# Shared keys and values in a windowed attention: two passes of the weighted sum, scores in one piece, and the lower halves of the weights made by accumulating transfers

## Chip, cores and metric

One NeuronCore of a Trainium2 chip runs the whole program in one launch. The metric is the device time of one execution in microseconds (us); the median of the runs shown counts. All data are float32.

## What is computed

Two hybrid layers and then one block of another kind, on 512 tokens of width 1024. Nearly all of the work is products with weight matrices. The part that the change rewrites is the windowed attention of the two hybrid layers: 16 query heads of 64 columns share 4 heads of keys and values (four query heads each), and a block of 128 queries sees its own block of keys and its two neighbours:

```
q = rms_norm(z_q.reshape(B, S, 16, 64)); k = rms_norm(z_k.reshape(B, S, 4, 64))   # then rotary on 16 columns
s = einsum('bnqhgd,bnjhd->bhgnqj', qb, kwin) / 8        # kwin: blocks n-1, n, n+1
s = where(|kpos - qpos| <= 128 and inside, s, -1e30)
m = max(max(s), sink); p = exp(s - m); p = p / (sum(p) + exp(sink - m))
o = einsum('bhgnqj,bnjhd->bnqhgd', p, vwin) * silu(gate)
```

## The kernel before

**Products.** TensorE multiplies in a rounded form of float32 (float32r). So that little is lost, each operand x is split into a high part hi (x rounded) and a low part lo = x - hi, and a product is three matmuls into the same PSUM tile: hi by hi, hi by lo, lo by hi. `mm3` does that; its three lines are L172, L173 and L174. Moving operands are 512 columns wide nearly everywhere.

**Weights.** All weight matrices come as a stream of 509 chunks of 128 rows by 1024 columns (512 KB), in the order of their use. `_load_raw` has the SyncE queue (SP) fetch one into a buffer `raw`; `_split_next` makes `hi` by a copy on ScalarE (ACT, L149) and `lo` by a subtraction on VectorE (DVE, L150). Each of `raw`, `hi` and `lo` has WB = 3 buffers, and `take`, called for each block of weights, keeps the splitting two chunks ahead of the use. A chunk holds eight blocks, and one block with 512 moving columns is three matmuls, so a chunk is 24 matmuls of 512 columns in most stages ("the steady rate"). Where a stage works on two token tiles only (`halves` in `tm`, the first tiles in `norm_tokens`, `down`), a chunk is used up in half of that or less. Some chunks (`HOLD`) are split into other tiles and kept.

**Attention.** For each layer there are two cores, one for each half g of the heads. `att_core` goes through eight steps, (n, pp) for the four query blocks n and two groups of four heads. A step issues: the weighted sum of the step before last (V, `mm3` with both heads of the half in one tile of 128 columns, three matmuls for each key block, results `pi`), the transposes of the step before (L771, four for each key block, results `pi`), and the scores of this step (L792, twelve matmuls of 64 rows; two that follow each other use the upper and the lower 64 rows of the array, results `pa`), then the masked maximum (L794, DVE), four exponentials (L223, ACT), and the scaling (L217 on DVE, L223 on ACT). There are 2, 3, 3 and 2 key blocks for the four n. PSUM has four `pa` banks, two `pi` banks and two `pm` banks. `weave` lets one unit of other work (one call of `fm`, 24 matmuls into `pm`: the first product of the convolution branch) go before each step. In the second core of a layer, filter taps of the convolution (`conv_taps`, DVE, L213) run along in the background.

**Order.** A scheduler orders each engine's instructions by the order of the program and by what it reckons to be ready; each engine then works through its own list in that order, waiting at semaphores. `issue_after(i)` adds the rule that an instruction of the same engine comes behind i in that list.

Of the kernel before, what the change touches and what calls it, by code (L numbers as in the profile page):

```python
# [10 lines left out]
F32 = mybir.dt.float32  # L11
F32R = mybir.dt.float32r
# [53 lines left out]


class Kern:
    def __init__(self, ctx, tc, ap):
# [21 lines left out]
        self.first = {}  # L91
        self.bg = None
# [39 lines left out]
    def _split_next(self):  # L132
# [36 lines left out]

    def mm3(self, out, lh, ll, rh, rl, start, stop):  # L170
# [3 lines left out]
        T.matmul(out, lhsT=ll, rhs=rh, start=False, stop=stop)  # L174

    def fm(self, key, cols, rhs, blocks=None, ts=None, pool=None):
# [4 lines left out]
        for k, (rh, rl) in enumerate(rhs):  # L181
# [3 lines left out]
            self.mm3(ps, wh, wl, rh, rl, k == 0, k == len(rhs) - 1)  # L185
# [489 lines left out]

    def att_kv(self, l, xg, xs):
# [3 lines left out]
        self.rms_h(xs, self.vk("norm_g", l), range(KT // 2))  # L680
        self.av = []
        for i in range(2):
            h, lo = self.slot(F32R), self.slot(F32R)
            for j in range(2):
                t = 2 * i + j
                c = slice(j * 256, j * 256 + 256)
                r = self.r[:, t:t + 1]
                self.act(h[:, c], ps[t][:, 256:512], AF.Copy, scale=r)
                self.stt(lo[:, c], ps[t][:, 256:512], r, h[:, c].bitcast(F32), ALU.mult, ALU.subtract)
            self.av.append((h, lo))  # L690
# [6 lines left out]
    def att_kT(self, nrm, ks):  # L697
        yield from nrm
        self.kT = []
        for p in range(2):  # L700
            self.kT.append(self.att_T(ks, p))
            yield
# [36 lines left out]
    def att_core(self, l, g):  # L739


        T = self.T
        qT, kT, av, sg = self.qT, self.kT[g], self.av, self.asg
        by_b = lambda x: x.rearrange("q (b p) -> q b p", b=2)
        sink, nsink = (by_b(x[:, 8 * g:8 * g + 8]) for x in (self.vk("sink", l), self.nsink))
        ya = [self.slot() for _ in range(4)]
        iters = [(n, pp) for n in range(NT) for pp in range(2)]
        hss = [slice(0, 64), slice(64, 128)]
        s1, s2 = {}, {}
        for it in range(len(iters) + 2):  # L750
            if 0 <= it - 2:
                n, pp = iters[it - 2]
                pt = s2.pop(it - 2)
                ps = self.misc()
                for x, (jb, ph, pl) in enumerate(pt):
                    c = (jb % 2) * 256 + g * 128
                    vh, vl = av[jb // 2]
# [795 lines left out]
```

## Time and profile before

| what | value |
|---|---|
| median of 3 runs | 3069.0 us (3067.52 to 3069.83) |
| profiled execution, its own time | 3067.16 us |
| its span, first to last instruction | 3065.4 us |
| TensorE clock granted over the span | 0.998 of full speed |
| PE busy | 3022.8 us |
| DVE busy | 2078.2 us |
| ACT busy | 1130.5 us |
| POOL (GpSimd) | 0.2 us, 4 instructions |
| HBM traffic | 94 GB/s over the span |

PE is TensorE's matmuls, PEld its weight loads. Matmuls overlap in the pipeline, so one is listed as taking about 0.39 us although the next one starts much sooner; what a matmul costs is read from the starts in the timeline. Idle time of an engine other than the one that sets the end costs nothing by itself. Some matmul records can be missing from a trace, so a group's count can be a few short; the counts of matmuls that matter are worked out from the loops.

### The profile page before, as it was taken

Reading aid. Unit: us, or ns where it says so; the run is one execution under the profiler, and the core shown is the slowest. Engines: PE = TensorE matmul, PEld = TensorE weight load, DVE = VectorE, ACT = ScalarE, POOL = GpSimd, SP = SyncE. Lnnn points to the kernel's source line nnn. Section 1 sums busy time; section 2 is a strip of 40 time slices with the busy share of each in tenths; the row PEclk is TensorE's granted clock in tenths of the full one; section 3 lists DMA queues with packets and bytes.
Section 4 is the critical chain, followed back from the end, with each engine's and each line's share of the span. In section 5 each row is a group of like instructions: output and inputs, shape, how many; then the busy total and the mean of one; then the engine's idle time right before and its main releaser. Section 6 shows DMA issues by size and latency. Waiting matters only on the chain.

```text
span 3065.4 us, 36069 instructions
## 1 busy us (share of the span) xinstructions
PE 3022.8 (99%) x13996; PEld 2470.4 (81%) x13996; DVE 2078.2 (68%) x3787; ACT 1130.5 (37%) x1783; POOL 0.2 (0%) x4
## 2 busy tenths in 40 slices
PE   8999999999999999999999999999999999999998
PEld 6777888887888877788888788887888888788887
DVE  7778897877444776889787764467776754753326
ACT  4545223334233444532333433333543332422222
POOL 0000000000000000000000000000000000000000
PEclk9999999999999999999999999999999999999999
DMA  4121322221233321122222132254222223422234
GB/s 163 63 69 49 97 89 76 83 76 63 95 98 129 117 76 62 62 83 97 71 74 76 63 103 96 97 173 143 90 90 69 65 74 123 161 96 99 98 110 151
DMA packets 83980, 288.99 MB, mean 94 GB/s; under 512 B 9440, under 2 KB 9696, under 8 KB 83680
## 3 DMA queue, kind: packets, MB, share of 16 engines
q1 hardware_dynamic: 83808, 286.68, 28.3%
q8 instruction: 110, 1.80, 0.2%
q14 instruction: 62, 0.51, 0.1%
HBM read 282.45 MB, written 4.19 MB: 94 GB/s over the span
## 4 chain that ended last, share of the span: by engine, by line
PE 90%; DVE 7%; ACT 2%; issue 1%; DMA 1%; SPq 0%; DVEq 0%; ACTq 0%
PE pm L172 20%; PE pm L174 20%; PE pm L173 20%; PE pa L172 6%; PE pa L174 6%; PE pa L173 6%; DVE lo L150 1%; DVE s L213 1%; PE pi L771 1%; PE pa L792 1%; PE pi L172 1%; DVE s L210 1%; PE pi L174 1%; PE pi L173 1%; ACT s L223 1%
## 5 line engine op out<-in xcount | busy, mean ns | idle before, releaser
L172 PE MATMUL pm<-s,hi 128*128 128x512 f32 x2848 | 1115.1, 392 | 1.9 <-ACT hi L149 1.2
L173 PE MATMUL pm<-s,hi 128*128 128x512 f32 x2848 | 1113.9, 391 | 0.0
L174 PE MATMUL pm<-s,lo 128*128 128x512 f32 x2848 | 1110.7, 390 | 0.5 <-DVE lo L150 0.5
L149 ACT CAST hi<-raw 128x1024 fp32r<-128x1024 f32 x497 | 523.2, 1053 | 1394.4 <-PE pm L173 761.2
L150 DVE TENSOR_TENSOR lo<-raw,hi 128x1024 fp32r<-128x1024 f32 x500 | 610.1, 1220 | 491.0 <-ACT hi L149 485.4
L172 PEld LDWEIGHTS pm<-s,hi 128*128 128x128 f32 x2848 | 534.5, 188 | 117.1 <-issue 3.5
L174 PEld LDWEIGHTS pm<-s,lo 128*128 128x128 f32 x2848 | 534.7, 188 | 113.1 <-issue 2.2
L173 PEld LDWEIGHTS pm<-s,hi 128*128 128x128 f32 x2848 | 534.8, 188 | 110.1 <-issue 1.7
L213 DVE SCALAR_TENSOR_TENSOR s<-s,m,s 128x497 f32<-128x497 f32 (+10 forms) x528 | 390.2, 742 | 11.4
L172 PE MATMUL pa<-hi,s 128*128 128x512 f32 x830 | 329.2, 397 | 9.3 <-ACT hi L147 6.7
L173 PE MATMUL pa<-lo,s 128*128 128x512 f32 x830 | 326.9, 394 | 4.8 <-DVE lo L150 4.8
L174 PE MATMUL pa<-hi,s 128*128 128x512 f32 x830 | 325.6, 393 | 0.0
L213 DVE SCALAR_TENSOR_TENSOR s<-s,pm 128x512 f32<-128x512 f32 x164 | 112.0, 683 | 147.4 <-PE pm L174 147.0
L172 PEld LDWEIGHTS pa<-hi,s 128*128 128x128 f32 x830 | 156.8, 189 | 43.0 <-ACT hi L147 6.7
L173 PEld LDWEIGHTS pa<-lo,s 128*128 128x128 f32 x830 | 157.1, 189 | 38.3 <-DVE lo L150 7.5
L174 PEld LDWEIGHTS pa<-hi,s 128*128 128x128 f32 x830 | 156.8, 189 | 31.8
L205 ACT CAST s<-s 128x512 fp32r<-128x512 f32 x184 | 110.4, 621 | 178.8 <-DVE s L213 139.1
L206 DVE TENSOR_TENSOR s<-s,s 128x512 fp32r<-128x512 f32 x184 | 123.0, 687 | 29.0 <-ACT s L205 28.2
L210 DVE TENSOR_TENSOR s<-s,s 128x512 f32<-128x512 f32 (+2 forms) x178 | 114.1, 662 | 1.7
L223 ACT ACTIVATE s<-s 128x512 f32<-128x512 f32 (+1 forms) x130 | 79.4, 628 | 89.9 <-DVE s L210 25.2
L223 ACT ACTIVATE s<-pa,m 128x256 f32<-128x256 f32 (+2 forms) x136 | 69.3, 524 | 77.4 <-DVE m L213 74.7
L213 DVE SCALAR_TENSOR_TENSOR s<-s,s 128x512 f32<-128x512 f32 (+1 forms) x130 | 88.1, 685 | 7.8 <-ACT s L223 6.3
(155 smaller groups left out, 2376.2 us busy)
## 6 DMA issues: line engine op xcount, KB each, us to landing
raw<-w SPq DMA_DIRECT2D x509, 512.0 KB, 3.3
s<-xT SPq DMA_DIRECT2D x16, 256.0 KB, 5.4
xd<-s SPq DMA_DIRECT2D x8, 256.0 KB, 2.0
s<-xd SPq DMA_DIRECT2D x8, 256.0 KB, 5.7
out<-s SPq DMA_DIRECT2D x8, 256.0 KB, 2.8
s<-c_ln_g SPq DMA_DIRECT2D x6, 256.0 KB, 4.4
s<-c_ln_b SPq DMA_DIRECT2D x6, 256.0 KB, 4.9
ckt<-ck SPq DMA_DIRECT2D x1, 1344.0 KB, 6.3
```

What stands on the lines that cost most here:

```text
L149: self.A.copy(h, raw)
L150: self.V.tensor_tensor(out=l, in0=raw, in1=h.bitcast(F32), op=ALU.subtract)
L172: T.matmul(out, lhsT=lh, rhs=rh, start=start, stop=False)
L173: T.matmul(out, lhsT=lh, rhs=rl, start=False, stop=False)
L174: T.matmul(out, lhsT=ll, rhs=rh, start=False, stop=stop)
L205: self.A.copy(h, src)
L206: self.V.tensor_tensor(out=l, in0=src, in1=h.bitcast(F32), op=ALU.subtract)
L210: return self.V.tensor_tensor(out=out, in0=a, in1=b, op=op)
L213: return self.V.scalar_tensor_tensor(out=out, in0=a, scalar=s, in1=b, op0=op0, op1=op1)
L223: return self.A.activation(out, a, f, bias=bias, scale=scale, **kw)
L771: T.transpose(ps[:, i * 128:i * 128 + 128], pr[i][:, x * 128:x * 128 + 128], self.ck("ident"))
L792: T.matmul(ps[:, 0:w], lhsT=a[hs, ns], rhs=b[hs, j0:j1], start=first, stop=last)
```

## The change

1. **Keys and values.** Values are laid out per token tile as [hi | lo] for each head (64 + 64 columns), so one weight tile of 128 columns holds both parts of one head. The weighted sum then takes two matmuls for each key block instead of three (weights [hi | lo] by the high part and by the low part of the probabilities); its upper and lower 64 rows are added afterwards by ACT copies and DVE additions into a new tile `y`. A step is now one of the four key/value heads (n, kv) with its four query heads. Keys are written twice (`twice`), so that either half of the array's rows holds the same head; four tiles of keys are transposed per layer instead of two.
2. **Order.** `behind` puts each score matmul and each transpose of a core behind the one issued before it, the scores behind the last weighted sum (`dense`), and the next unit of other work behind the transposes. The transposes of the step before now come after the scores.
3. **Weights.** For the 426 chunks in `ADDED`, ACT writes `lo` = float32r(-raw), which is -hi, and a transfer issued by POOL adds `raw` to it in place (`accum_op=add`). The DVE subtraction is left out for them.

```
+A_1, A_2 = C_OUT + 8 + 2 * (8 - KEEP_0) + 8, C_O + 8 + 2 * (8 - KEEP_1) + 8
+ADDED = {*range(6, C_OUT - 3), *range(A_1, C_O - 3), *range(A_2, NCHUNK - FT - 3)}
...
+            if c in ADDED:
+                self.act(l, raw, AF.Copy, scale=-1.0)
+                self.nc.gpsimd.dma_start(out=l, in_=raw, accum_op=ALU.add)
...
-            self.V.tensor_tensor(out=l, in0=raw, in1=h.bitcast(F32), op=ALU.subtract)
+            if c not in ADDED:
+                self.V.tensor_tensor(out=l, in0=raw, in1=h.bitcast(F32), op=ALU.subtract)
...
+    def behind(self, on=True):
+        return self.tc.issue_after(self.pe.ins) if on and self.pe is not None else nullcontext()
...
+            with self.behind(k == 0):
+                self.mm3(ps, wh, wl, rh, rl, k == 0, k == len(rhs) - 1)
...
+            for i in range(2):
+                self.A.copy(yr[:, :, i, :], xr)
...
+        ks, self.kT = self.twice(ks), []
+        for p in range(4):
...
-                    self.mm3(ps, vh[:, c:c + 128], vl[:, c:c + 128], ph, pl, x == 0, x == len(pt) - 1)
+                    v = av[jb][:, c:c + 128]
+                    T.matmul(ps, lhsT=v, rhs=ph, start=x == 0, stop=False)
+                    self.dense = T.matmul(ps, lhsT=v, rhs=pl, start=False, stop=x == len(pt) - 1)
+                y = self.slot()
+                for u in range(2):
+                    cs, o = slice(u * 256, u * 256 + 256), hss[1 - u]
+                    self.A.copy(y[hss[u], 0:256], ps[o, cs])
+                    self.tt(y[hss[u], 0:256], y[hss[u], 0:256], ps[hss[u], cs], ALU.add)
+                for x in range(2):
+                    p = 2 * kv + x
+                    self.stt(ya[p][:, ns], sg[p][:, ns], 0.5, y[:, x * 128:x * 128 + 128], ALU.mult, ALU.mult)
...
+                self.pe = self.dense
...
+                            with self.behind():
+                                self.pe = T.matmul(ps[:, 0:w], lhsT=a[hs, ns], rhs=b[hs, j0:j1], start=first, stop=last)
```

How the order of instructions moves, at three places. In the tile names, `pi`, `pa`, `pm` are PSUM tiles, `s` general tiles, `ckt` the constants (here the identity for transposes).

PE before, first core of layer 0, a middle step (n = 1): the end of a weighted sum, then scores with transposes among them.

```order
L174 MATMUL pi_1166<-s_1088,s_364 128x512
L792 MATMUL pa_1206<-s_665,s_847 128x384
L792 MATMUL pa_1207<-s_665,s_847 128x384
...
L792 MATMUL pa_1216<-s_665,s_856 128x384
L771 MATMUL pi_1177<-ckt,s_1118 128x128
L771 MATMUL pi_1177<-ckt,s_1119 128x128
...
L792 MATMUL pa_1217<-s_665,s_856 128x384
L792 MATMUL pa_1216<-s_666,s_856 128x384
```

Each change between scores and transposes here is a place where the stream of matmuls changes its kind; over the four cores the scores stand in 80 separate runs.

PE after the change, the same kind of step: two groups of transposes follow the whole piece of scores, then 24 matmuls of other work, then the third group of transposes, and right behind it the weighted sum whose last two matmuls need that group.

```order
L784 MATMUL pi_1323<-s_1286,s_369 128x512
L813 MATMUL pa_1339<-s_682,s_867 128x384
...
L813 MATMUL pa_1350<-s_682,s_877 128x384
L847 MATMUL pi_1378<-ckt,s_1247 128x128
...
L847 MATMUL pi_1387<-ckt,s_1250 128x128
L186 MATMUL pm_1405<-s_341,hi_1176 128x512
...
L847 MATMUL pi_1396<-ckt,s_1250 128x128
L783 MATMUL pi_1439<-s_1383,s_363 128x512
...
L783 MATMUL pi_1439<-s_1401,s_369 128x512
L784 MATMUL pi_1439<-s_1402,s_369 128x512
```

The scores now stand in 32 runs of twelve, and the third group of transposes has moved to the front of the weighted sum that needs it; PE has 64 instructions fewer in all.

ACT after the change, in the retention stage: the two passes over a chunk (`hi` and the negated `lo`) stand around the evacuation (`pm`) of a unit; before, only the `hi` pass stood there.

```order
L157 CAST hi_4841<-raw_4675 128x1024
L238 ACTIVATE s_4809<-pm_4777 128x512
L238 ACTIVATE lo_4842<-raw_4675 128x1024
L220 CAST s_4824<-s_4822 128x512
L157 CAST hi_4904<-raw_4728 128x1024
```

The transfer that completes `lo_4842` is the next thing in POOL's list, which holds nothing else.

PE after the change, in the second block's first product, where the chunks of the first half go at twice the rate and chunk 326 is the first of the second half to be made by a transfer. Between the last use of the buffer that its `lo` takes over (`lo_17284`) and the first use of `lo_17351` there are 19 matmuls.

```order
L187 MATMUL pa_17188<-lo_17284,s_16961 128x512
L187 MATMUL pa_17187<-lo_17333,s_16991 128x512
...
L188 MATMUL pa_17188<-hi_17332,s_16996 128x512
L186 MATMUL pa_17416<-hi_17350,s_16949 128x512
L187 MATMUL pa_17416<-lo_17351,s_16949 128x512
```

Between these two places `lo_17351` has to be written by ACT and completed by its transfer; before, it was written by DVE alone.

## Rows read from the trace of the kernel before

**Rows 1.** The page's first part: the span, and of each engine the busy time, its share of the span and its instructions.

```profile
span 3065.4 us, 36069 instructions
PE 3022.8 (99%) x13996; PEld 2470.4 (81%) x13996; DVE 2078.2 (68%) x3787; ACT 1130.5 (37%) x1783; POOL 0.2 (0%) x4
```

**Rows 2.** The timeline of PE in a dense stretch: start, duration, engine, line, operation, tiles, size. The second row shown is the 24th matmul after the first; the 23 between them are left out.

```profile
600.04 0.39 PE L172 MATMUL pm<-s,hi 128*128 128x512 f32 x1
...
605.49 0.39 PE L172 MATMUL pm<-s,hi 128*128 128x512 f32 x1
```

**Rows 3.** Windows of chosen stretches: stretch, its length, then busy time and instructions of PE, PEld, DVE, ACT and POOL, the granted clock, the DMA share and GB/s. The first, second, fourth and fifth are the four attention cores, from the first score to the last weighted sum; the third is a stretch with convolution taps in the background; the sixth is the recurrent stage of the second block.

```profile
90.10:171.60 81.50, 79.57 (x421) 61.43 (x421) 57.12 (x174) 47.93 (x122) 0.00 (x0) 1.00 0.16 52
219.30:302.50 83.20, 82.62 (x427) 62.98 (x427) 68.73 (x193) 48.04 (x122) 0.00 (x0) 1.00 0.15 53
310.00:690.00 380.00, 379.97 (x1700) 313.52 (x1699) 320.67 (x488) 117.77 (x158) 0.00 (x0) 1.00 0.26 84
1106.20:1187.80 81.60, 79.68 (x421) 61.46 (x421) 57.20 (x174) 47.98 (x122) 0.00 (x0) 1.00 0.16 52
1235.50:1318.70 83.20, 82.60 (x426) 62.91 (x426) 68.66 (x193) 48.02 (x122) 0.00 (x0) 1.00 0.16 52
2250.00:2500.00 250.00, 245.77 (x1318) 202.33 (x1317) 166.60 (x336) 92.14 (x132) 0.00 (x0) 1.00 0.21 70
```

**Rows 4.** Groups by line and shape in the second core, 219.3 to 302.5 us: line, engine, operation, tiles, size, count, busy time and mean of one, idle time before them and its releasers.

```profile
L771 PE MATMUL pi<-ckt,s 128*128 128x128 f32 x80 | 13.1, 284 | 0.6 <-DVE s L217 0.3
L792 PE MATMUL pa<-s,s 64*128 64x384 f32 x48 | 8.9, 390 | 0.0
L792 PE MATMUL pa<-s,s 64*128 64x256 f32 x48 | 5.3, 312 | 0.0
L205 ACT CAST s<-pi 128x512 fp32r<-128x512 f32 x20 | 11.4, 587 | 11.7 <-PE pi L771 11.7
L206 DVE TENSOR_TENSOR s<-pi,s 128x512 fp32r<-128x512 f32 x20 | 13.5, 688 | 2.4 <-ACT s L205 2.1
L223 ACT ACTIVATE s<-pm 128x512 f32<-128x512 f32 x4 | 2.4, 588 | 0.0
```

**Rows 5.** The timeline of PE in a middle step of the second core: scores and transposes in pieces (a merged row stands for xcount instructions, the start is that of the first).

```profile
245.88 0.79 PE L792 MATMUL pa<-s,s 64*128 64x384 f32 x6
246.77 0.57 PE L771 MATMUL pi<-ckt,s 128*128 128x128 f32 x3
247.26 0.44 PE L792 MATMUL pa<-s,s 64*128 64x384 f32 x1
247.63 0.33 PE L771 MATMUL pi<-ckt,s 128*128 128x128 f32 x1
```

**Rows 6.** The timeline of PE ahead of the first core and around its first scores, which stand in one piece already; the first row is eight transposes of the same size as those of L771.

```profile
86.39 1.03 PE L673 MATMUL pi<-ckt,s 128*128 128x128 f32 x8
...
89.77 0.39 PE L174 MATMUL pm<-s,lo 128*128 128x512 f32 x1
90.09 0.97 PE L792 MATMUL pa<-s,s 64*128 64x256 f32 x12
90.99 0.50 PE L172 MATMUL pm<-s,hi 128*128 128x512 f32 x1
91.33 0.40 PE L173 MATMUL pm<-s,hi 128*128 128x512 f32 x1
```

**Rows 7.** The timeline of PE in windows of a few hundredths of a microsecond inside the six scores at 245.88: the starts of the second and the third pair.

```profile
246.16 0.51 PE L792 MATMUL pa<-s,s 64*128 64x384 f32 x4
246.32 0.34 PE L792 MATMUL pa<-s,s 64*128 64x384 f32 x2
```

**Rows 8.** The timeline of PE at the end of the first core, where the next product into `pa` begins.

```profile
160.88 0.73 PE L792 MATMUL pa<-s,s 64*128 64x256 f32 x7
...
165.49 0.50 PE L172 MATMUL pa<-hi,s 128*128 128x512 f32 x1 [1.04 <-ACT s L223]
```

**Rows 9.** The timeline of DVE in a middle step of the first core: the subtraction of a chunk, and the first masked maximum behind the scores.

```profile
107.06 1.23 DVE L150 TENSOR_TENSOR lo<-raw,hi 128x1024 fp32r<-128x1024 f32 x1 [0.27 <-ACT hi L149]
109.52 0.56 DVE L794 CUSTOM_DVE_ANT_0 pa<-pa,ckt 128x384 f32<-128x384 f32 x1
```

**Rows 10.** The timeline of ACT in the same step: the first exponential and the last two scalings.

```profile
111.91 0.59 ACT L223 ACTIVATE s<-pa,m 128x384 f32<-128x384 f32 x1 [3.73 <-DVE m L213]
...
115.34 1.12 ACT L223 ACTIVATE s<-s,m 128x384 f32<-128x384 f32 x2
```

**Rows 11.** DMA: the SP queue's packets, megabytes and share of the 16 engines' span; and issues with their size and the median time to landing.

```profile
q1 hardware_dynamic: 83808, 286.68, 28.3%
raw<-w SPq DMA_DIRECT2D x509, 512.0 KB, 3.3
ckt<-ck SPq DMA_DIRECT2D x1, 1344.0 KB, 6.3
```

**Rows 12.** The costliest groups of the whole span: the two halves of the splitting of weights, and the filter taps.

```profile
L149 ACT CAST hi<-raw 128x1024 fp32r<-128x1024 f32 x497 | 523.2, 1053 | 1394.4 <-PE pm L173 761.2
L150 DVE TENSOR_TENSOR lo<-raw,hi 128x1024 fp32r<-128x1024 f32 x500 | 610.1, 1220 | 491.0 <-ACT hi L149 485.4
L213 DVE SCALAR_TENSOR_TENSOR s<-s,m,s 128x497 f32<-128x497 f32 (+10 forms) x528 | 390.2, 742 | 11.4
```

**Rows 13.** Who PE waited for: line that waited with its tile, releaser, us in total, times, longest.

```profile
PE pa L173 <- DVE lo L150: 4.8, 5, 1.9
```

More of the change, by code (lines that the diff above doesn't have):

```diff
@@ L1 @@
 import math
-from contextlib import ExitStack
+from contextlib import ExitStack, nullcontext
 import numpy as np
@@ L91, in __init__ @@
         self.first = {}
+        self.pe = None
         self.bg = None
@@ L173, in mm3 @@
         T.matmul(out, lhsT=lh, rhs=rl, start=False, stop=False)
-        T.matmul(out, lhsT=ll, rhs=rh, start=False, stop=stop)
+        self.dense = T.matmul(out, lhsT=ll, rhs=rh, start=False, stop=stop)
     def fm(self, key, cols, rhs, blocks=None, ts=None, pool=None):
@@ L674, in att_T, with twice @@
         return self.split(ps)
+    def twice(self, xs):
+        out = []
+        for x in xs:
+            y = self.slot()
+            yr, xr = y.rearrange("p (h x d) -> p h x d", x=2, d=64), x[:, 0:256].rearrange("p (h d) -> p h d", d=64)
+            for i in range(2):
+                self.A.copy(yr[:, :, i, :], xr)
+            out.append(y)
+        return out
     def att_kv(self, l, xg, xs):
@@ L681, in att_kv @@
         self.av = []
[L682 to L690, printed above, removed]
+        for t in range(NT):
+            v, r = self.slot(F32R), self.r[:, t:t + 1]
+            vr = v.rearrange("p (h x d) -> p h x d", x=2, d=64)
+            pv = ps[t][:, 256:512].rearrange("p (h d) -> p h d", d=64)
+            self.act(vr[:, :, 0, :], pv, AF.Copy, scale=r)
+            self.stt(vr[:, :, 1, :], pv, r, vr[:, :, 0, :].bitcast(F32), ALU.mult, ALU.subtract)
+            self.av.append(v)
         ks = []
@@ L742, in att_core @@
         T = self.T
[L743 to L745 removed]
+        qT, av, sg = self.qT, self.av, self.asg
         ya = [self.slot() for _ in range(4)]
[L747 removed]
+        iters = [(n, kv) for n in range(NT) for kv in range(2)]
         hss = [slice(0, 64), slice(64, 128)]
@@ L791, in att_core @@
                         for ps, hs in zip(both, hss):
-                            T.matmul(ps[:, 0:w], lhsT=a[hs, ns], rhs=b[hs, j0:j1], start=first, stop=last)
+                            with self.behind():
+                                self.pe = T.matmul(ps[:, 0:w], lhsT=a[hs, ns], rhs=b[hs, j0:j1], start=first, stop=last)
                     for i in (x, 2 + x):
@@ L814, in att_core @@
                 s1[it] = pr
+            if 0 <= it - 1 < len(iters):
+                n, kv = iters[it - 1]
+                pr = s1.pop(it - 1)
+                j0 = max(0, n - 1)
+                pt = []
+                for x in range(min(NT, n + 2) - j0):
+                    ps = self.misc()
+                    for i in range(4):
+                        with self.behind():
+                            T.transpose(ps[:, i * 128:i * 128 + 128], pr[i][:, x * 128:x * 128 + 128], self.ck("ident"))
+                    h, lo = self.split(ps)
+                    pt.append((j0 + x, h, lo))
+                s2[it - 1] = pt
             yield
+        self.pe = None
         self.ya += [self.split(y) for y in ya]
@@ L1534 @@
             mats[n, l] = x[n][l]
-        order = np.array([8 * g + 4 * (i % 2) + i // 2 for g in range(2) for i in range(8)])
-        idx = (order[:, None] * 64 + np.arange(64)[None, :]).reshape(-1)
-        mats["aq", l] = x["w_in"][l][:, O_AQ + idx]
-        mats["ag", l] = x["w_in"][l][:, O_AG + idx]
-        mats["ao", l] = x["w_attn_out"][l][idx]
+        mats["aq", l] = x["w_in"][l][:, O_AQ:O_AQ + D]
+        mats["ag", l] = x["w_in"][l][:, O_AG:O_AG + D]
+        mats["ao", l] = x["w_attn_out"][l]
     for n in ("w_in_2", "w_a_2", "w_b_2", "w_o_2", "w_ffn_gate_2", "w_ffn_up_2", "w_ffn_down_2", "w_ple_2",
```

40 lines of the change are left out of this document (12 added, 28 removed).

## Prediction

> **What bounds the kernel now.** The page's first part comes first [rows 1]: of a span of 3065.4 us PE is busy 3022.8 and idle 42.6, while DVE, ACT and POOL have time to spare. So the time is the length of the stream of matmuls, and a change counts if it shortens that stream or makes it wait. The busy figure hides one thing: a matmul listed at 0.39 us starts every 0.227 us (24 starts from 600.04 to 605.49, 5.45 us) [rows 2]. A matmul of 512 columns is therefore priced at **0.227**, and a chunk of weights at the steady rate at 5.45.
>
> Next come the windows [rows 3]. The four cores last 81.5, 83.2, 81.6 and 83.2 us, 329.5 together. What should they take? In the second, of 427 matmuls 80 are transposes and 96 are scores [rows 4]; the other 251 are 512 wide: 251 x 0.227 = 57.0. Eight transposes in a row take 1.03, the last of them 0.28 [rows 4, 6], so one starts every (1.03 - 0.28) / 7 = 0.107; 80 are 8.6. Scores run in pairs, one in each half of the array, a pair 0.16 apart at 384 columns (246.16 to 246.32) [rows 7], and I take 0.115 at 256 columns, by width: 24 x 0.165 + 24 x 0.115 = 6.7. Together 72.3. The core takes 83.2, so **10.9 us are lost, while PE is listed as busy** (82.62): the loss is in the starts. The first core (245 wide matmuls, 70.9) loses 10.6; all four some 43. In a middle step one sees where [rows 5]: six scores, three transposes, one score, one transpose; the piece 247.26 to 247.63 is a lone score of 0.37, more than twice its pair price. The first scores of a core stand in one piece already [rows 6]: entry 90.09 - 89.77 = 0.32 instead of 0.227 (+0.09), twelve in 0.90 instead of 6 x 0.115 = 0.69 (+0.21), exit 91.33 - 90.99 = 0.34 (+0.11): **0.41 us lost for a piece of twelve**.
>
> **The change, part by part.** The sum is made against the execution's own 3067.2 us; the median of the runs lies 1.8 above it.
>
> *A, two passes.* Key blocks are 2 + 3 + 3 + 2 = 10 for each of two steps, 20 products per core, 80 in all, one matmul fewer each: 80 x 0.227 = **-18.1**. All on PE, so it counts in full, unless waits take it back (D, E).
>
> *B, scores in one piece.* Eight pieces of twelve per core at 0.41 are 3.3; I add 1.0 for changes to and from transposes, which now stand in whole groups and which no row shows apart. So 10.8 on the mean becomes 4.3, 6.5 less per core: **-26**. Bounds: 0, if the loss isn't from the interleaving but from something that stays (waits for `pa` banks), and -43, if all goes.
>
> *C, the third group of transposes* now stands right ahead of the weighted sum that reads it. Its results need an ACT copy of 0.59 and a DVE subtraction of 0.69 [rows 4]; with handovers and sometimes a weight pass of 1.05 ahead on ACT [rows 12] that is 1.3 to 2.3. The four matmuls of the first two key blocks cover 0.91. I take a wait of 0.9, three times per core by the order: 12 x 0.9 = **+11** (0 to 16). Before, work stood between, and the transposes idled 0.6 in a whole core [rows 4].
>
> *D, the end of each layer's first core.* The next product takes the `pa` banks of the last step. Before, PE went from those scores at 160.88 to that product at 165.49 and idled 1.04 for an exponential [rows 8]. Now 8 transposes and 14 wide matmuls (4.1) plus the sum lie between, but maxima, then four exponentials, run as before: in a middle step from 109.52 [rows 9] to 111.91 + 4 x 0.59 = 114.3 [rows 10], 4.8. With the new copies in front on ACT I take 1.5 more, twice: **+3** (0 to 6).
>
> *E, the end of the second core.* The last weighted sum is followed closely by products that read it, now through two copies, two additions, two scalings and a split (0.6 to 0.7 each, side by side on two engines [rows 4]); +1.5 twice, **+3** (0 to 5). In the middle of a core the same steps, 8 x 2 copies of about 0.4, lie beside 24 wide matmuls and cost nothing; ACT is at 48 of 83 there [rows 3].
>
> *F, sixteen more transposes* of keys: 16 x 0.107 = **+1.7**. The doubled writes are ACT's, beside dense work.
>
> *G, the transfers.* Each of 426 chunks loses a DVE pass of 1.22 [rows 9, 12], 520 us of an engine that PE seldom waits for (4.8 us in five waits [rows 13]): gain near zero. It gains an ACT pass of 1.05 (+448 on an engine at 37% [rows 1]) and a transfer. The condition: the buffer is freed by the last use of chunk c - 3, and by the order of PE two chunks and two matmuls later chunk c is read, 50 x 0.227 = 11.35 us. ACT may need the other pass, one copy of 0.59 and the negation first, 1.05 + 0.59 + 1.05 = 2.7. **The transfer has 8.6 us.** No row shows an accumulating one. From below: a plain load of the same 512 KB lands in 3.3; from above: one that moves 1344 KB, near the 1536 KB of two readings and a writing, 6.3 [rows 11]. I take 6, nearer the upper end, since it must read both sides. It fits by 2.6 us, at cost zero. Traffic: the queues are at 28.3% with 286.68 MB [rows 11]; 426 x 0.524 = 223 MB add 22 points for each passage, 72% with two and 95% with three: tight, not full. Where chunks go faster just before, it doesn't fit: chunks 326 and 426 have 19 matmuls, 4.3 us, against 1.05 + 6 and the ones behind them 8: **+5** for both (0 to 10).
>
> *H, the rest.* In the recurrent stage (250 us with 4.2 idle [rows 3]) DVE is lighter by some 250 / 5.45 = 46 passes, and half of the idle time may go, **-2** (-6 to +3); norm stages, with ACT fuller, **+1**.
>
> Sum: -18.1 - 26 + 11 + 3 + 3 + 1.7 + 5 - 2 + 1 = **-21.4**, 3045.8 of the execution's own time, 3047 as a median.
>
> **The rivals.** *R1, slower: the transfer doesn't fit its slot.* Three buffers make it a loop: use, negation, transfer, use; each us beyond 8.6 is paid once in three chunks, 426 / 3 = 142 us. At 9.6 us the time is 3067 - 21 + 142 = 3188; the sign turns at 8.75. For it: the traffic of 95%, a queue of POOL in which one transfer's start waits behind the former's semaphores, and descriptor writing for which there is no row. Against it: even the 1344 KB load has 2.3 us to spare. *R2, slower: DVE holds POOL's transfers back.* In the stretch with taps DVE is busy 320.67 of 380 us [rows 3] in passes of 0.742 [rows 12]; if the parts of a start have to slip in between them, four passes (my choice) are 3.0; 6.3 + 3.0 = 9.3 is 0.7 beyond the slot, 0.23 for each of 2 x 380 / 5.45 = 139 chunks in both layers: -21 + 32 = +11, 3078. Against it: no transfer of POOL stands in this trace to show it. The Trainium skill (SBUF — State Buffer, SBUF: two separate sides, the note on the "DVE blocks DMA" trap) has such a rule: while DVE runs in a mode that takes two ports, the descriptors of GpSimd's transfers can't be written, and a transfer of some 620 ns took 3100 ns; by it the time would be that of R2. It speaks of fast modes. The passes here take 1.22 for 1024 columns, 0.742 for 497 and 0.688 for 512 [rows 4, 12], none at twice the rate of another, so I leave R2 at 0.06. *R3, no change: the pieces' gain is eaten by waits.* Scores in one piece need all `pa` banks free at once, so PE would wait for the exponentials; for it: from the first maximum to the last scaling are 109.52 to 115.34 + 1.12 = 116.5, 7.0 us [rows 9, 10], of a step of 81.5 / 8 = 10.2; then B is -8 instead of -26 and C 16, 3069, same. Against it: 24 wide matmuls (5.45) follow every piece. *R4, more gain: no new waits*, C to E and G zero: 3067 - 43 = 3024.
>
> **How the numbers follow.** Forecast 0.60, its own range 3030 to 3060 (B and C between their bounds). R1 0.12, R2 0.06, R3 0.14, R4 0.08. Of R1 a mild part, up to 8.85 us (36 - 21 = +14), falls below 3085; the range 3024 to 3085 thus leaves out most of R1 (0.10) and the part of R4 below 3024 (0.04), and 0.06 for what I haven't seen. What one can tell from no change is 0.2%, 6 us. Faster: forecast 0.58 and R4 0.08, 0.66; same 0.14; slower 0.20 (R1, R2, and a forecast that loses to larger waits).
>
> **What would show it.** The two lines of the weighted sum with 80 rows each where three had 80; scores in runs of twelve; cores of about 74 to 76 us from first score to last weighted sum; transfers to `lo` landing in 6 us, at most 8.6; PE's waits naming no transfer in dense stretches, a few us at chunks 326 and 426; waits of PE for the split of the third transposes below 1 us. The forecast is wrong if dense stretches no longer start a matmul each 0.227 us, or if the cores stay above 79.

## The result and the profile after

The changed kernel takes **3095.0 us** (median of 4 runs, 3092.24 to 3096.94), before 3068.3 (4 runs); the ratio is 1.0084 with the interval [1.0071, 1.0097]. It is slower by 27 us, where 21 less were forecast. The profiled execution has a span of 3092.2 us against 3065.4 [rows 1]: 26.8 to explain.

The first part of the page of the changed kernel:

```profile
span 3092.2 us, 36918 instructions
PE 3013.5 (97%) x13932; PEld 2451.5 (79%) x13932; DVE 1626.1 (53%) x3365; ACT 1553.4 (50%) x2293; POOL 367.5 (12%) x430
```

PE is busy 9 us less than before and idle 79 instead of 43. DVE lost 452 us and ACT gained 423. The windows of the changed kernel that answer to [rows 3] (the cores moved by the shift of the program):

```profile
91.50:176.70 85.20, 78.29 (x412) 58.98 (x412) 50.48 (x164) 59.34 (x143) 6.88 (x8) 0.98 0.43 106
222.30:308.50 86.20, 80.09 (x421) 59.07 (x420) 58.29 (x178) 61.02 (x146) 7.74 (x9) 1.00 0.47 111
1115.30:1198.90 83.60, 76.71 (x411) 57.89 (x411) 50.44 (x164) 59.33 (x143) 6.88 (x8) 1.00 0.46 112
1244.50:1330.80 86.30, 80.13 (x421) 59.10 (x420) 58.39 (x178) 61.10 (x147) 7.75 (x9) 1.00 0.47 112
310.00:690.00 380.00, 379.22 (x1685) 311.35 (x1684) 260.66 (x433) 173.71 (x218) 50.75 (x59) 1.00 0.69 161
2250.00:2500.00 250.00, 248.30 (x1342) 207.64 (x1342) 132.08 (x303) 126.50 (x168) 29.45 (x34) 1.00 0.63 150
```

The second and the fourth of these windows run on to the start of the next product, 1.0 us behind the last weighted sum. From the first score to the last weighted sum the four cores last 85.2, 85.2, 83.6 and 85.3 us, not 74 to 76, with 80 weighted-sum matmuls fewer. The dense stretch from 310 to 690 is as full as it was (379.22 of 380), 24 wide products in it still start in 5.44 us (from 600.19), and PE waits there for no transfer, while the DMA share rose from 0.26 to 0.69. So the transfers do no harm at the steady rate.

Where the 26.8 us lie is seen best by counting the 11208 wide products with weights in both traces and subtracting the start of the same product. This table is worked out that way; the first row is the start before, the others the shift against it, for the changed kernel and for the experiments that follow.

```
product no.          300    950   4000   4650   7450   7700   9000   9450   9600  last
start before        87.2  317.2 1091.2 1323.5 2082.6 2141.7 2514.1 2653.2 2689.5 3053.8
changed             +0.8   +5.6   +9.2  +10.1   +9.7  +16.0  +11.8  +11.4  +26.0  +26.8
e1_att              +3.1  +14.5  +15.8  +24.9  +24.6  +24.7  +25.2  +24.9  +24.9  +24.9
e2_xfer             +2.3   +0.8   +4.8   +2.9   +4.4  +11.2   +9.1   +8.9  +21.7  +21.9
f2_loads            +0.9   -0.6   +2.7   +0.8    0.0   +1.0   -3.2   -3.3   +6.7   +6.9
e6_edges            +2.6   +1.0   +3.1   +1.3   +2.3   +6.4   +2.9   +2.2  +11.5  +11.5
e8_late             +4.5    0.0   +1.4   -3.5   -5.2   -5.1   -5.1   -5.3   -5.3   -5.3
h3_mid              +3.4   -7.0   -0.7  -12.7  -11.8  -12.9  -16.9  -17.4  -14.4  -13.2
```

The attention of the two layers lies between products 300 and 950 and between 4000 and 4650: +4.8 and +0.9, **+5.7** where the prediction's terms A to F said -25.4. Two short places of the second block (7450 to 7700 and 9450 to 9600) cost +6.3 and +14.6, **+20.9** where +5 was said. Between, 760 us of dense products cost -0.4.

A part of this is TensorE's clock. In four stretches the granted clock is at half (1.2 instead of 2.4 GHz), where the kernel before has it at full in the same work; the number behind the five engines is the granted clock:

```profile
167.30:170.60 3.30, 3.30 (x9) 2.57 (x8) 2.24 (x6) 2.17 (x7) 0.00 (x0) 0.50 0.50 159
310.70:314.00 3.30, 3.30 (x8) 2.00 (x8) 1.39 (x3) 1.66 (x3) 0.00 (x0) 0.50 0.47 159
2676.10:2679.40 3.30, 3.30 (x9) 2.53 (x8) 0.00 (x0) 0.00 (x0) 0.00 (x0) 0.50 1.03 235
2703.40:2713.60 10.20, 5.87 (x14) 4.61 (x15) 1.36 (x2) 1.24 (x2) 0.00 (x0) 0.50 0.49 166
```

Each time PE had just waited: 1.3 and 0.9 us ahead of the first stretch, 1.0 ahead of the second, 2.8 ahead of the third; the fourth begins inside a wait of 5.9. At half clock a wide product starts every 0.427 us instead of 0.227:

```profile
2711.74 0.63 PE L186 MATMUL pa<-hi,s 128*128 128x512 f32 x1
2712.16 0.63 PE L187 MATMUL pa<-lo,s 128*128 128x512 f32 x1
```

The 40 products in these stretches, each 0.20 late, make some 8 of the 26.8 us (an estimate from these rows): 3.4 of the attentions' 5.7 and 4.6 of the 14.6. One more such stretch lies at 2075 us before and at 2099 after, on either side of product 7450, so that some 1.5 us of the +6.3 belong to the row before it.

Who PE waited for in the changed kernel (line with its tile, releaser, us in total, times, longest):

```profile
PE pi L847 <- DVE s L225: 10.3, 21, 1.3
...
PE pa L186 <- ACT s L220: 5.9, 1, 5.9
PE pi L783 <- DVE s L221: 5.5, 16, 0.4
PE pa L187 <- DMA lo<-raw: 5.2, 3, 2.8
PE pi L847 <- DVE s L221: 5.0, 12, 0.5
...
PE pi L1017 <- DVE s L1246: 3.6, 1, 3.6
```

L847 are the transposes, L783 the weighted sum, L225 additions (of halves among them), L220 and L221 the split. The first, third and fifth of the rows shown are new waits in the cores; the second, the sixth and nearly all of the fourth are the two short places. The two rows left out, 6.5 us for a `hi` and 4.1 for a `lo`, have their like before (6.7 and 4.8).

**A middle step of a core.** PE in the first core, without the wide products that stand between (start, duration, engine, line, operation, tiles, size, idle before):

```profile
116.90 1.34 PE L813 MATMUL pa<-s,s 64*128 64x384 f32 x12
118.17 0.66 PE L847 MATMUL pi<-ckt,s 128*128 128x128 f32 x4
...
119.76 0.63 PE L847 MATMUL pi<-ckt,s 128*128 128x128 f32 x4 [0.47 <-DVE s L225]
...
125.78 0.66 PE L847 MATMUL pi<-ckt,s 128*128 128x128 f32 x4 [0.37 <-DVE s L221]
126.80 0.50 PE L783 MATMUL pi<-s,s 128*128 128x512 f32 x1 [0.37 <-DVE s L221]
...
128.67 1.31 PE L813 MATMUL pa<-s,s 64*128 64x384 f32 x12
```

and ACT in the same step:

```profile
117.61 0.37 ACT L789 COPY s<-pi 64x256 f32<-64x256 f32 x1
118.65 0.36 ACT L789 COPY s<-pi 64x256 f32<-64x256 f32 x1 [0.68 <-DVE s L225]
121.48 0.58 ACT L238 ACTIVATE s<-pa,m 128x384 f32<-128x384 f32 x1 [2.47 <-DVE m L228]
...
123.82 0.59 ACT L220 CAST s<-pi 128x512 fp32r<-128x512 f32 x1
...
125.46 0.56 ACT L220 CAST s<-pi 128x512 fp32r<-128x512 f32 x1
125.93 1.06 ACT L238 ACTIVATE lo<-raw 128x1024 fp32r<-128x1024 f32 x1
126.89 0.57 ACT L220 CAST s<-pi 128x512 fp32r<-128x512 f32 x1
```

The scores stand in one piece of 1.27 us (116.90 to 118.17), as forecast. But there are two `pi` banks. One holds the weighted sum until its halves are copied and added, so the second group of transposes waits (0.47). The first group is transposed at 118.17, yet its copy for the split stands in ACT's list *behind* the exponentials, at 123.82; its bank is held for over 7 us, the third group can only start at 125.78, its copy comes behind a negation at 126.89, and the weighted sum waits twice. The step takes 11.8 us.

**The place at 2700.** SP's list in the changed kernel, the stall that ended, and what SP waited for from 2630 to 2720:

```profile
2700.23 0.33 SPq L132 DMA_DIRECT2D raw<-w  x1
2700.61 1.69 SPq L1322 DMA_DIRECT2D s<-pT  x2
```

```profile
2707.06 1.28 ACT L220 CAST s<-s 128x512 fp32r<-128x512 f32 x2 [6.01 <-DMA s<-pT]
```

```profile
SPq L132 <- DMA lo<-raw: 48.5, 8, 16.0
```

A buffer `raw` is now read by the transfer, not by a DVE pass, and is free only when that has landed. SP's next load of weights waits for it (48.5 us in eight waits), and the small load `pT` behind it in the same list waits too: it was issued at 2700.61, and PE waited 5.9 us for its split. Before, this load went out at 2679.30, ahead of any need. The wait at L1017 is of the same kind: its releaser, a memset, wrote into a tile that such a small load had filled.

### The profile page after: what moved, and what is told of

It is laid out like the page before. It is cut to its first block, busy times and chain, and to the rows that moved or that the text cites. A ratio compares the mean times of both kernels' runs of the same rounds, so it can differ in the third digit from the quotient of the medians.

```text
span 3092.2 us, 36918 instructions
## 1 busy us (share of the span) xinstructions
PE 3013.5 (97%) x13932; PEld 2451.5 (79%) x13932; DVE 1626.1 (53%) x3365; ACT 1553.4 (50%) x2293; POOL 367.5 (12%) x430
## 3 DMA queue, kind: packets, MB, share of 16 engines
q0 software_dynamic: 61344, 223.37, 39.4%
q1 hardware_dynamic: 83808, 286.68, 28.3%
## 4 chain that ended last, share of the span: by engine, by line
PE 81%; DVE 10%; ACT 4%; DMA 3%; issue 2%; SPq 0%; POOL 0%; DVEq 0%; ACTq 0%; POOLq 0%
PE pm L187 18%; PE pm L188 18%; PE pm L186 18%; PE pa L187 6%; PE pa L186 6%; PE pa L188 6%; DVE s L228 2%; ACT s L238 2%; DVE s L225 2%; DVE pa L815 1%; DMA lo<-raw 1%; DVE s L221 1%; ACT s L220 1%; DMA raw<-w 1%; DVE m L228 1%
## 5 line engine op out<-in xcount | busy, mean ns | idle before, releaser
L152 POOL DMA_DIRECT2D lo<-raw x426 | 367.3, 862 | 2622.7 <-ACT lo L238 2269.3
L238 ACT ACTIVATE lo<-raw 128x1024 fp32r<-128x1024 f32 x426 | 448.8, 1054 | 153.1 <-PE pa L187 137.6
L228 DVE SCALAR_TENSOR_TENSOR s<-s,pm 128x512 f32<-128x512 f32 x164 | 112.4, 685 | 585.2 <-PE pm L188 368.7
L228 DVE SCALAR_TENSOR_TENSOR s<-s,m,s 128x497 f32<-128x497 f32 (+10 forms) x528 | 390.3, 743 | 18.2 <-DMA s<-c_gm_g 5.0
L187 PEld LDWEIGHTS pa<-lo,s 128*128 128x128 f32 x830 | 158.5, 191 | 44.3 <-DMA lo<-raw 6.5
L221 DVE TENSOR_TENSOR s<-s,s 128x512 fp32r<-128x512 f32 x184 | 123.7, 689 | 98.3 <-ACT s L220 96.6
L220 ACT CAST s<-s 128x512 fp32r<-128x512 f32 x184 | 110.1, 616 | 75.8 <-DVE s L228 56.7
L159 DVE TENSOR_TENSOR lo<-raw,hi 128x1024 fp32r<-128x1024 f32 x74 | 90.0, 1217 | 104.0 <-ACT hi L157 103.0
L228 DVE SCALAR_TENSOR_TENSOR s<-s,s 128x512 f32<-128x512 f32 (+2 forms) x194 | 104.3, 556 | 71.8 <-ACT s L238 70.0
L225 DVE TENSOR_TENSOR s<-s,s 128x512 f32<-128x512 f32 (+2 forms) x178 | 114.2, 662 | 4.6 <-ACT s L317 2.5
```

Source lines behind the costliest of these rows:

```text
L152: self.nc.gpsimd.dma_start(out=l, in_=raw, accum_op=ALU.add)
L187: T.matmul(out, lhsT=lh, rhs=rl, start=False, stop=False)
L220: self.A.copy(h, src)
L221: self.V.tensor_tensor(out=l, in0=src, in1=h.bitcast(F32), op=ALU.subtract)
L225: return self.V.tensor_tensor(out=out, in0=a, in1=b, op=op)
L228: return self.V.scalar_tensor_tensor(out=out, in0=a, scalar=s, in1=b, op0=op0, op1=op1)
```

## The experiments

All are timed against the kernel before on the same chip; a ratio is to it. "Loss" is, over the four cores, the time between starts beyond the prediction's prices of single starts, up to the start behind the last weighted sum: 44.3 us before and 62.4 after the change. Time at half clock inside a core counts as loss too.

**Which part.** e1_att makes no chunk by a transfer, e2_xfer puts the transfers alone on the old attention:

```
-ADDED = {*range(6, C_OUT - 3), *range(A_1, C_O - 3), *range(A_2, NCHUNK - FT - 3)}
+ADDED = set()                                          # e1_att; e2_xfer is the kernel before with the hunk on ADDED
```

> The attention part and its order alone: no chunk is made by a transfer (ADDED empty), all else as after the change. Theory: the attention itself is slower, because the result bank of the weighted sum is now emptied by copy, add, copy, add (some 2.5 us from its last matmul) before the second group of transposes can use it, and the first group waits behind the exponentials on ACT; alignment of the two traces put about +10 us on the two attention stages. So before + 5 to + 12 us (3073 to 3080), cores 83 to 86 us, and PE's waits of the transposes on DVE still about 10 us in all. Rival: the new ACT passes of the weights, queued ahead of the copies and splits on ACT, make these waits; then without them the forecast of the sum holds for this part, before - 15 to - 25 us (3043 to 3053), cores 74 to 77 us.

Measured: 3092.3, ratio 1.0076 [1.0063, 1.0089], loss 79.0. Both theories miss: the attention costs +23, more than the table's +5.7, so without the transfers it is worse. PE's waits show why; for the splits (L221) they are 28 us instead of 10.7:

```profile
PE pi L783 <- DVE s L221: 10.1, 18, 1.6
PE pi L784 <- DVE s L221: 9.7, 16, 0.8
PE pi L847 <- DVE s L221: 8.2, 16, 0.9
PE pi L847 <- DVE s L225: 7.8, 21, 1.2
```

With the subtraction back on DVE, the splits come later still: in a middle step of e1_att a subtraction of weights (1.23 us from 129.42) stands right ahead of the third group's split (130.56). The transfers thus do not make these waits, they ease them.

> The accumulating transfers alone, on the attention of the kernel before. Theory: nothing in the dense stretches, + 4 at the first transferred chunk of the second block's middle (chunk 326), + 14 to 15 around chunk 426 (of which about 6 are a small load that stands in SP's queue behind loads whose buffer is still being read by a transfer), some -2 to -3 in the recurrent stage, and 0 to + 4 in the attention cores from the negations on ACT: before + 14 to + 20 us (3082 to 3088). Rival (the attention makes those late places late too, or the transfers hurt everywhere): under + 8, or over + 25 us.

Measured: 3084.7, ratio 1.0049 [1.0036, 1.0063], as the theory said. By the table the cores gain a little (loss 40.1) and nearly all lies in the two short places. The two parts alone make +23 and +15, together +27: they aren't additive.

**Is it the order?** e4_twopass takes e1_att, makes `behind` do nothing and issues the transposes ahead of the scores, as before the change; e3_noorder only makes `behind` do nothing:

```
-        return self.tc.issue_after(self.pe.ins) if on and self.pe is not None else nullcontext()
+        return nullcontext()
```

> The two passes of the weighted sum alone: no transfers, no order rules, transposes issued ahead of the scores of a step as in the kernel before. Theory of the result bank (copy, add, copy, add hold it): the waits stay though the pieces are back, so the 18 us of the shorter sum are mostly given back: before - 8 to + 6. Rival, that the order rules make all the waits: before - 14 to - 18 us, as many microseconds as matmuls left out.

Measured: 3067.5, ratio 0.9994 [0.9985, 1.0003], loss 53.8. The two passes alone give back nearly all of the 18 us of the shorter sum, as the theory said. That the bank is the reason is not shown: PE's waits at these transposes (L803 in that kernel) come to 8.3 us, only 2.5 of them for additions, and half clock from 167 and from 1181 us takes some 4 (estimated as above).

> As the attention part alone, but the scheduler is free (the order rules issue nothing); the transposes are still written behind the scores. If the order rules cost more in waits than they save in pieces, this is faster than the attention part alone by 3 to 10 us; if they save their 26 us, it is slower by 10 or more; theory: within 8 us of it, since 6.4 us per core saved in pieces stand against 10 us of waits of which the bank's part stays.

Measured: 3065.3, ratio 0.9989 [0.9980, 0.9998], loss 52.6: 27 us faster than e1_att, far more than any of the three expected. In this order of the program the order rules cost more in waits than they save. They need not: e8_late, below, keeps them with another place of the splits and is 6.5 us faster than e3_noorder.

**Which wait.** On the changed kernel, g1_copies issues both copies ahead of both additions; g2_late issues the transposes and splits of the step before ahead of a step's maxima and exponentials; g3_late_copies does both:

```
-                for u in range(2):
-                    cs, o = slice(u * 256, u * 256 + 256), hss[1 - u]
-                    self.A.copy(y[hss[u], 0:256], ps[o, cs])
-                    self.tt(y[hss[u], 0:256], y[hss[u], 0:256], ps[hss[u], cs], ALU.add)
+                cs = [slice(u * 256, u * 256 + 256) for u in range(2)]
+                for u in range(2):
+                    self.A.copy(y[hss[u], 0:256], ps[hss[1 - u], cs[u]])
+                for u in range(2):
+                    self.tt(y[hss[u], 0:256], y[hss[u], 0:256], ps[hss[u], cs[u]], ALU.add)
...
             if it < len(iters):          # g2_late: only the score matmuls here
+            if 0 <= it - 1 < len(iters): # transposes and splits of the step before, moved up
...
+            if it < len(iters):          # then maxima, exponentials, scalings
```

> The changed kernel with one edit: of each weighted sum both copies of halves are issued first and both additions after them (before: copy, addition, copy, addition). In the trace after, the second copy stood waiting for the first addition 20 times, 11.7 us in all, and the second group of transposes waited for the second addition to leave the bank. Theory (the bank of the weighted sum is held too long): - 5 to - 11 us against the changed kernel (3084 to 3090), the transposes' wait for additions (10.3 us) at half or less. Rival (the engines' whole load in a step sets its length): the wait moves to the splits, within 3 us of the changed kernel (3092 to 3098).

Measured: 3103.3, ratio 1.0112 [1.0096, 1.0127], loss 68.2. Neither: it is slower by 8. The wait for additions fell from 10.3 to 8.5 us only, and the ones for splits rose. A part of the 8 us is the clock (0.992 to 0.995 of full in its four runs, 0.994 to 0.995 in those of the changed kernel). The serial copies were not what held the step.

> The changed kernel with one edit: in a step the transposes of the step before and their splits are issued ahead of the maxima and exponentials of the step, so that on ACT the copies that split stand ahead of the exponentials instead of behind them; TensorE's order keeps its rules. Theory (the first group's bank waits behind four exponentials, so the third group and the weighted sum wait for the splits): - 8 to - 16 us against the changed kernel (3079 to 3087), and the waits of transposes and weighted sums for the splits (10.5 us) near zero. Rival (the softmax is the loop that sets the step): its chain gets 1.4 us longer, no change or up to + 10 us.

Measured: 3074.3, ratio 1.0019 [1.0009, 1.0028], loss 44.3: 21 faster than the changed kernel, more than expected, and PE's waits in the cores for splits fell from 10.7 to 0.5 us; the one for additions rose to 18.4. In a middle step the first group's bank, held for 7.6 us after the change, is free again after at most 4.4 (transposes from 119.91, the third group from 124.28).

> Both edits on the changed kernel. Theory: they act on different waits, so - 14 to - 26 us against the changed kernel (3069 to 3081), cores 78 to 82 us. Rival (one loop, which either edit only shifts): no better than the better of the two alone.

Measured: 3073.5, ratio 1.0014 [1.0005, 1.0024], loss 41.8: no better than g2_late within the intervals. So the place of the splits in the engines' lists is the cause, and the copies' order counts for little beside it. With the splits of ACT and DVE the edit moves the third group of transposes on PE, from the front of the weighted sum into the unit; no run moves one of the three alone, so their shares are not known.

**Without the transfers.** e8_late is e1_att with the edit of g2_late.

> The attention part with its order rules, without transfers (the subtraction is DVE's again), with the one edit that moves a step's splits ahead of its maxima and exponentials. Theory (what the transfers gave in the cores was room on DVE, and where the splits stand in the engines' lists is the larger part of the waits): 18 to 26 us faster than the attention part alone (3092), at 3066 to 3075. Rival (DVE's load alone makes the waits, the place in the list counts only with the transfers): within 8 us of it, 3084 to 3095.

Measured: 3058.8, ratio 0.9962 [0.9948, 0.9976], loss 47.3: 33 us faster than e1_att by an edit that lets the splits go first (on PE the third group of transposes moves forward within the unit with it), and past what the theory expected. Some 6 of its loss of 47.3 are half clock, from 166 and from 1180 us. ACT of e8_late in a middle step:

```profile
122.82 0.59 ACT L220 CAST s<-pi 128x512 fp32r<-128x512 f32 x1
125.22 0.21 ACT L238 ACTIVATE m<-m 128x4 f32<-128x4 f32 x1 [1.82 <-DVE m L225]
125.34 0.57 ACT L220 CAST s<-pi 128x512 fp32r<-128x512 f32 x1
126.70 0.59 ACT L220 CAST s<-pi 128x512 fp32r<-128x512 f32 x1 [0.80 <-PE pi L823]
127.19 0.59 ACT L238 ACTIVATE s<-pa,m 128x384 f32<-128x384 f32 x1
```

All three copies now stand ahead of the step's exponentials, which begin at 127.19. And with this order the transfers cost what they cost alone: g2_late is 15.5 above e8_late, e2_xfer 15.2 above the kernel before, alike within the intervals. What they eased in the cores was thus most likely this one jam.

**The two short places.** f2_loads is e2_xfer with the second block's small loads issued by POOL; e6_edges is e2_xfer with the two later ranges beginning two chunks later:

```
-            self.nc.sync.dma_start(pt[i], self.ap["pT"][i])        # and the same in load2
+            self.nc.gpsimd.dma_start(pt[i], self.ap["pT"][i])      # f2_loads
...
-A_1, A_2 = C_OUT + 8 + 2 * (8 - KEEP_0) + 8, C_O + 8 + 2 * (8 - KEEP_1) + 8
+A_1, A_2 = C_OUT + 8 + 2 * (8 - KEEP_0) + 10, C_O + 8 + 2 * (8 - KEEP_1) + 10   # e6_edges
```

> The transfers alone on the old attention, with the few small loads of the second block (its constants and the input of the last product) issued by POOL instead of SP. Theory (they stood in SP's queue behind loads of weights whose buffer a transfer was still reading; the late one at the end cost 5.8 us, the one before the second product some 3 to 5): 7 to 11 us faster than the transfers alone (3074 to 3078). Rival (the loads are late because the DMA engines are full, or the waits are hidden ones for the weights): within 3 us of the transfers alone (3082 to 3088).

Measured: 3074.6, ratio 1.0018 [1.0009, 1.0028]: 10.1 faster than e2_xfer (9.5 by the ratios, each to its own chip). By the table the first place goes from +6.8 to +1.0: its wait for the memset, 4.7 us in e2_xfer, is gone. At the second, the waits from 2640 to 2720 have lost the 5.8 us for a split (of `pT`) that stood first in those of e2_xfer:

```profile
PE pm L179 <- ACT hi L155: 3.0, 1, 3.0
PE pa L180 <- DMA lo<-raw: 2.8, 1, 2.8
```

But this place goes from +12.8 to +10.0 only: around the end of either wait that is left TensorE falls to half clock, from 2659.6 to 2666.4 and from 2686.9 to 2693.7. In e2_xfer one such stretch lay there, and the wait for `pT` filled nearly half of it.

> The transfers alone on the old attention, but the two later ranges begin two chunks later (at 328 and 428 instead of 326 and 426), so that no transfer has less than two chunks of matmuls between the release of its buffer and its use. Theory: the wait for a transfer and what follows it there (2 to 4 us at 326, 3 to 5 at 426) goes, the queued small loads (about 10 us) stay: 4 to 8 us faster than the transfers alone (3077 to 3081). Rival (the loads of weights themselves are late there, whatever chunk begins): within 2.5 us of the transfers alone.

Measured: 3078.7, ratio 1.0035 [1.0022, 1.0048]: 6.0 faster than e2_xfer (4.3 by the ratios, whose intervals overlap), and in the same stretch no wait for a transfer is left; the wait for `pT`, 5.6, is:

```profile
PE pa L179 <- ACT s L212: 5.6, 1, 5.6
PE pm L179 <- ACT hi L155: 3.0, 1, 3.0
```

Ten and four to six make the 15, within the noise.

**Versions with all of it.** h1_free is the changed kernel without order rules, h2_late is g3_late_copies, both with the edits of f2_loads and e6_edges. h3_mid is h2_late with the transposes called six matmuls into the next unit:

```
     def fm(...):
         for k, (rh, rl) in enumerate(rhs):
+            if k == 2:
+                self.run_hook()      # transposes and splits of the step before, then exponentials and scalings
```

> The changed kernel, no order rules, small loads issued by POOL, later ranges two chunks later. Sum by the runs so far: attention without rules and without transfers - 4 against the kernel before; transfers relieve DVE in the cores (- 1 to - 2 each) and in the recurrent stage (- 3); what stays at the edges + 2: 3055 to 3063. If the gains don't add (the free scheduler places by its own reckoning): 3063 to 3070.

Measured: 3070.5, ratio 1.0011 [1.0001, 1.0021], loss 55.3: a miss, just above even the range for gains that do not add.

> The changed kernel with its order rules, splits ahead of the softmax and copies ahead of additions, small loads issued by POOL, later ranges two chunks later. Sum: 3073.5 of the variant with both edits of the attention, less 10 for the loads, less 4 to 6 for the edges: 3056 to 3062.

Measured: 3056.9, ratio 0.9963 [0.9950, 0.9976], loss 42.6, as expected.

> As the one before, but the transposes of a step stand six matmuls into the unit of other work behind the scores instead of directly behind the scores, with their splits behind the maxima and ahead of the exponentials. Theory (the bank of the weighted sum is emptied in some 2.5 us by two copies and two additions, and the transposes' second group waits for it 14 us in all): six matmuls, 1.4 us, cover most of it, 6 to 12 us faster than the one before, 3046 to 3054, waits of transposes for additions below 5 us. Rival (the softmax's chain, now longer by two splits, becomes the wait): no gain, or up to + 10.

Measured: **3054.9**, ratio 0.9957 [0.9942, 0.9972], loss 36.4; 13 us faster than the kernel before. Against h2_late it is 2 us, not 6 to 12, and the intervals overlap. Its PE goes from the scores into other work, and the first two groups of transposes follow without a wait:

```profile
117.82 1.32 PE L822 MATMUL pa<-s,s 64*128 64x384 f32 x12
119.08 0.50 PE L191 MATMUL pm<-s,hi 128*128 128x512 f32 x1
...
120.56 1.03 PE L839 MATMUL pi<-ckt,s 128*128 128x128 f32 x8
...
123.71 0.66 PE L839 MATMUL pi<-ckt,s 128*128 128x128 f32 x4 [0.95 <-DVE s L228]
...
128.64 1.32 PE L822 MATMUL pa<-s,s 64*128 64x384 f32 x12
```

The wait for additions fell from 13.9 us in h2_late to 2.0; the third group now waits 0.95 for a split (L228 in that kernel). In all, PE's waits for these splits rose from 3.2 to 9.5 us, which takes back half of that gain.

h4_mid_sub is h3_mid with no chunk made by a transfer.

> The best version so far (transposes six matmuls into the unit, splits ahead of the exponentials, copies ahead of additions) with no chunk made by a transfer, so that DVE subtracts for all of them. If the transfers are worth DVE's room even there, + 4 to + 12 us against it (3059 to 3067); if a good order makes room enough, within 3 us (3052 to 3058); if the transfers only cost (edges, start, norm stages), 3 to 6 us faster than it (3049 to 3052).

Measured: 3058.8, ratio 0.9965 [0.9952, 0.9978], loss 45.6. That is 3.9 us above h3_mid (2.5 by the ratios), but the intervals overlap: what the transfers are worth in a good order, a few us or nothing, is not settled.

## Why the prediction was wrong

- **A, two passes: right as a count.** The weighted sum has 80 matmuls fewer, 18 us of PE. Alone they brought some 2 (e4_twopass, 3067.5 beside 3069.5 of the kernel before on that chip): the prediction added "unless waits take it back", and did not allow enough for that.
- **B, scores in one piece: right in kind, a bit too large.** Summing the losses at starts next to a score, the four cores had 30.8 us before and 11.0 after: -20, where -26 was said.
- **C, the step that failed.** The prediction let a wait arise at one place of a step, the third group's split, 0.9 us three times a core. The losses at all other starts went from 13.5 to 51.4 us, **+38, where C, D and E allowed 17**. The wait that it named was not too small: the weighted sums waited 5.7 us for splits, where 11 was said. What it put at nothing is the wait of the transposes themselves for a free `pi` bank, **15.3 us** (10.3 for the additions, 5.0 for the splits). It looked at how long the split takes, 0.59 and 0.69, and at what PE does meanwhile, but not at where the split stands in ACT's list: behind four exponentials, so that the first group's bank was held 7.6 us. With the splits ahead of them g2_late is 21 us faster. That place follows from the order of the program text, which the change turned over (scores and softmax ahead of the transposes), and it could be read in the order of ACT ahead of time. The prediction also took a `pi` bank to be free when the second group comes; it holds the weighted sum's halves. Of the rest of the 38, some 1.6 are half clock in the first core and 2.5 lie behind the second cores (E); what is left, waits too short to be listed and changes of kind, was not taken apart. Rival R3 named the right kind of loss, waits that eat what the pieces gave, but by `pa` banks and up to no change only; PE waited for `pi` banks.
- **The clock** has no term in the sum. Half clock behind the new waits cost some 8 us, and the prediction priced every wait at its own length.
- **D and E** belong to the same sum; E alone shows behind the second core of a layer, +2 to +3 (said +1.5).
- **G, right at the steady rate and wrong at the edges.** The transfer lands in 5.4 us where 6 was taken, within its 8.6, and dense stretches show no wait; the two queues take 67.7% of the engines' time where 72% was said. R1 and R2 did not come. The edges cost 20.9 instead of 5. The direct wait was sized about right (4.9 in PE's waits, 4 to 6 by e6_edges), the term that was missing is a queue: `raw` is held longer, SP's next load waits, and small loads behind it with it, some 10 by f2_loads. A part of the 20.9 is half clock, 4.6 at the second place. The prediction counted the slot of `lo` and forgot that of `raw`.
- **The two parts are not independent**, which the sum assumed: e1_att +23 and e2_xfer +15 make +27 together, because the transfers relieve DVE of 1.22 us per step just where the splits were late.
- **H**: the recurrent stage gained 4.2 (said 2), and the stages between the attentions of the layers lost 3.6 (said 1).

On R2: the Trainium skill (SBUF — State Buffer, SBUF: two separate sides, the note on the "DVE blocks DMA" trap) would have POOL's transfers held up while DVE works in a two-port mode. In the stretch from 310 to 690 us DVE is busy 260.66 of 380, and the transfers there land in 5.4 us as over the whole span; they were not held up. No row tells whether any of these passes runs in such a mode, so the rule itself is not tested here.

## What to carry to other kernels

When work is moved, read its new place in the lists of *all* engines that serve it: a matmul moved well can still leave the small copy that empties its bank behind a long chain on another engine, and here one edit of that place was worth 21 to 33 us. Whoever hands a buffer to a slower reader should ask who waits for the buffer next, and what stands behind that wait in the same queue: small late loads belong in another queue than the stream. Two changes that load the same engine must be timed apart and together; their sum says little. And a wait of TensorE can cost more than its length: look at the granted clock behind it before the time is put down to the wait.

## What the runs showed of the hardware

The DMA rows of the changed kernel that answer to [rows 11]:

```profile
q0 software_dynamic: 61344, 223.37, 39.4%
q1 hardware_dynamic: 83808, 286.68, 28.3%
raw<-w SPq DMA_DIRECT2D x509, 512.0 KB, 3.9
lo<-raw POOLq DMA_DIRECT2D x426, 512.0 KB, 5.4
```

An accumulating transfer of 512 KB within the chip's own memory lands in 5.4 us and is counted as one passage of its bytes, but takes the engines (39.4 / 223.37) / (28.3 / 286.68) = 1.8 times as long per byte as a load. The loads beside it land in 3.9 instead of 3.3, and POOL is listed busy 367.3 us for issuing 426 of them, 0.86 each. Behind waits of PE the granted clock was at half in four stretches of the changed kernel where it was at full before, and a wide product then started every 0.427 us instead of 0.227.
